# A fixed order for TensorE in an attention stage: one place a unit, transposes between projection steps

## The chip, the cores and the metric

The kernel runs on one core of a Trainium2 chip. The metric is the device time of one execution in microseconds (us); the figure of a kernel is the median of several executions. A profile is of one further execution, with its own time; its span runs from the first to the last instruction.

## The reference, cut to what matters

A trunk of two layers over 512 tokens of 1024 channels: a Mamba-2 mixer with a gated feed-forward, then differential attention with the same kind of feed-forward. The change lies in the attention alone:

```python
kv = rms_norm(x, kv_ln_g) @ kv_w                      # keys: 8 heads x 2 maps x 64; values: 8 x 128
k  = rms_norm(k, k_norm_g)
q  = rms_norm((rms_norm(x, ln_g) @ q_w).reshape(b, s, 8, 2, 64), q_norm_g)
for each block i of 128 queries, causal:
    logits = einsum('bqhcd,bkhd..', q, k) * scale + rel_bias[bucket(distance)]
    p = softmax(logits)
    attn = p[:, :, 0] - lam * p[:, :, 1]
    o = attn @ v
o = rms_norm(o, subln_g) * (1 - lam_init)
x = x + o @ attn_out_w
```

## The kernel before

The activations lie channel by token in `xgh[k]` and `xgl[k]` (k = 0 to 7, 128 channels each): every large product is made of three matmuls, high part by high, high by low and low by high, of 128 x 128 weights with 512 columns. Six projections, `k0 q0 v0 k1 q1 v1`, make the keys, queries and values of heads 0 to 3 (`0`) and 4 to 7 (`1`), and two output projections, `attn_out(0)` and `attn_out(1)`, bring the heads back into the stream. `proj` (L937) makes one projection for four blocks of 128 tokens, in four accumulators (the tag `mm` in PSUM, four banks), over four chunks of weights of two k each: 24 matmuls a chunk, 96 in all. `chunk` has the weights loaded (SyncE's queue) and split into high and low part (ScalarE and VectorE) two chunks ahead. For keys and queries, `qk` (L962) evacuates the blocks on ScalarE, squares and sums them, takes `rsqrt_act` (VectorE, ScalarE, VectorE), multiplies (L977, VectorE), and transposes the product on TensorE (`turned`, L980: 16 transposes, four a block), from which ScalarE writes `kT` or `qT` (L985).

The attention itself goes by units: a head has three, the query blocks 0 and 1 together, block 2, block 3. A unit has four steps. `logits` (L1009): matmuls of 64 rows for both maps into two banks, VectorE adds the bias and takes the maximum (L1034), ScalarE the exponential (L1042). `weigh` (L1045): VectorE makes the difference of the two maps. `turn` (L1058): TensorE transposes it into one bank, ScalarE copies it (`at`, L1064). `values` (L1066): TensorE multiplies with `vt` into one bank (`po`), ScalarE scales it into `ot` (L1077). Behind a head's last unit come `normed_out` (L1080: square, sum, `rsqrt_act`, product, L1087) and `turned_out` (L1089: four transposes into one bank `oT`, from which ScalarE makes `oh` and VectorE `ol`, L1097, the operands of the output projection). The small outputs share the tag `aux`, four banks.

What sets the order: the program is a tape. A planner orders each engine's instructions by when it holds them to be ready, with the program's order as preference, and hands out the banks of a tag as they come free. `heads` (L1101) is a generator that puts unit t's logits, unit t-2's transposes and unit t-3's values in one round, with a `yield` after each; `weave` runs projection or output steps (a step is 12 matmuls of a projection, or 12 of an output projection) at these yields. There are two runs of `heads`, over heads 0 to 3 and 4 to 7; the first runs empty before the second starts. Transposes of keys, queries and heads' outputs are put off into a list `pend` and issued by `pended`, behind the last matmul traced (`tc.issue_after`): for keys and queries inside the next projection, at its second chunk after two blocks, that is behind 36 matmuls. The bias table (`rb`, `oh`, `ps_rb`, L920 to L931) is traced ahead of all this; its buffers are those of the feed-forward before.

Of the kernel before, what the change touches and what calls it, by code (L numbers as in the profile page):

```python
# [39 lines left out]
def trunk_kernel(ctx: ExitStack, tc, x, ssm_ln_g, ssm_in_w, ssm_conv_w, ssm_conv_b, ssm_dt_bias,  # L40
# [16 lines left out]
    def mm_bank(name):  # L57
        return pp.tile([P, T], F32, tag="mm", name=name)
# [128 lines left out]
    def chunk(key):  # L187
        while state["next"] <= state["use"] + AHEAD and state["next"] < len(plan):
            emit_chunk()
        state["use"] += 1  # L190
        k, h, l = ready.pop(0)
        assert k == key, (k, key)
        return h, l

    def mm3(ps, wh, wl, xh, xl, start, stop):
        pe.matmul(ps, wh, xh, start=start, stop=False)  # L196
        pe.matmul(ps, wh, xl, start=False, stop=False)  # L197
        return pe.matmul(ps, wl, xh, start=False, stop=stop).ins  # L198
# [260 lines left out]
    def run(gen):  # L459
        for _ in gen:  # L460
            pass
# [438 lines left out]
    norm1 = Norm(bp, "f1")  # L900
    with tc.tile_pool(name="att_o", bufs=1) as op_, tc.tile_pool(name="att", bufs=1) as ap:
        rts = []
        pend = []

        def pended(age=0):

            with tc.issue_after(state["last"]):
                for p in list(pend):
                    if p[0] >= age:
                        pend.remove(p)  # L910
                        p[1]()
                    p[0] += 1

        def put_off(f):
            pend.append([0, f])


        rb = ap.tile([32, AH], F32, name="rb")
# [18 lines left out]
        def proj(key, evac):  # L937
            pss = [mm_bank("ps_%s_%d" % (key, b)) for b in range(NT)]
            for k0 in range(0, KB, 2):
                wh, wl = chunk("%s_%d" % (key, k0))  # L940
                for b in range(NT):
                    ts = slice(b * P, (b + 1) * P)
                    for k in range(k0, k0 + 2):
                        st, sp_ = k == 0, k == KB - 1
                        pe.matmul(pss[b], xgh[k][:, ts], wh[:, k - k0, :], start=st, stop=False)
                        pe.matmul(pss[b], xgh[k][:, ts], wl[:, k - k0, :], start=False, stop=False)
                        state["last"] = pe.matmul(pss[b], xgl[k][:, ts], wh[:, k - k0, :],
                                                  start=False, stop=sp_).ins
                    if b == 1:
                        if k0 == 2:  # L950
                            pended()
                        yield
                if k0 + 2 < KB:
                    yield
                if not rts:
                    tc.keep_in_program_order(act.preload_act_table_set("natural_log_exp_and_others"))
                    rts.append(norm_kv.col())
            for b in range(NT):
                evac(b, pss[b], rts[0])
            yield  # L960

        def qk(key, dst, gcol):  # L962
            kn, ss = [], ap.tile([P, NT, 8], F32, tag="qss", name="ss" + key, bufs=2)

            def evac(b, ps, rt):
                t = ap.tile([P, T], F32, tag="kn", name="kn%s_%d" % (key, b), bufs=4)
                s = ap.tile([P, T], F32, tag="ksq", name="ksq%s_%d" % (key, b), bufs=1)
                act.activation(t, ps, AF.Copy, scale=rt[:, b:b + 1])
                act.activation(s, t, AF.Square)
                dve.reduce_sum(ss[:, b, :], s.rearrange("p (a q) -> p a q", a=8), axis=AX.X)  # L970
                kn.append(t)

            yield from proj(key, evac)
            rsqrt_act(ss, ap, key, [P, NT, 8], 64)
            for b in range(NT):
                v = kn[b].rearrange("p (a q) -> p a q", a=8)
                dve.tensor_tensor(out=v, in0=v, in1=ss[:, b, :].unsqueeze(2).to_broadcast([P, 8, 64]),  # L977
                                  op=ALU.mult)

            def turned():  # L980
                for b in range(NT):
                    ps = aux_bank("kt%s_%d" % (key, b))
                    for h in range(4):
                        pe.transpose(ps[:, h * P:(h + 1) * P], kn[b][:, h * P:(h + 1) * P], ident)
                    act.activation(dst[:, :, b * P:(b + 1) * P], ps.rearrange("p (h t) -> p h t", h=4),  # L985
                                   AF.Copy, scale=c2[:, gcol:gcol + 1])

            put_off(turned)
            yield

        def vproj(key, i):
            def evac(b, ps, rt):
# [87 lines left out]
        def normed_out(h, st):  # L1080
            ot = st["ot"]
            sq = ap.tile([P, T], F32, tag="ksq", name="osq%d" % h, bufs=1)
            so = ap.tile([P, NT], F32, tag="so", name="so%d" % h, bufs=2)
            act.activation(sq, fl(ot), AF.Square)
            dve.reduce_sum(so, sq.rearrange("p (a q) -> p a q", a=NT), axis=AX.X)
            rsqrt_act(so, ap, "o%d" % h, [P, NT], P)
            dve.tensor_tensor(out=ot, in0=ot, in1=so.unsqueeze(2).to_broadcast([P, NT, P]), op=ALU.mult)  # L1087

        def turned_out(h, st):  # L1089
            ot = st["ot"]  # L1090
            ps = aux_bank("oT%d" % h)
            for i in range(NT):
                pe.transpose(ps[:, i * P:(i + 1) * P], ot[:, i, :], ident)
            oh_ = op_.tile([P, T], F32R, tag="oh", name="oh%d" % h, bufs=6)
            ol_ = op_.tile([P, T], F32R, tag="ol", name="ol%d" % h, bufs=6)
            act.activation(oh_, ps, AF.Copy, scale=c2[:, 50:51])
            dve.scalar_tensor_tensor(out=ol_, in0=ps, scalar=c2[:, 50:51], in1=oh_.bitcast(F32),  # L1097
                                     op0=ALU.mult, op1=ALU.subtract)
            return oh_, ol_

        def heads(hs, os):  # L1101

            us = []
            for h in hs:
                st = {}
                us += [Unit(h, part, st) for part in range(len(PARTS))]
            n = len(us)
            for t in range(n + 4):
                pended(1)
                if t < n:  # L1110
                    us[t].logits()
                    yield
                if 0 <= t - 1 < n:
                    us[t - 1].weigh()
                if 0 <= t - 2 < n:
                    us[t - 2].turn()
                    yield
                if 0 <= t - 3 < n:
                    us[t - 3].values()
                    yield  # L1120
                if 0 <= t - 4 < n and us[t - 4].part == len(PARTS) - 1:
                    normed_out(us[t - 4].h, us[t - 4].st)
                    put_off(lambda u=us[t - 4]: os.append(turned_out(u.h, u.st)))
                    yield

        def attn_out(i, os, norm):
            held = []
            for c in range(4):
                wh, wl = chunk("ao%d_%d" % (i, c))
                late = (2, 0, 0, 0)[c] if i else 0  # L1130
                pss = [mm_bank("ps_ao%d_%d" % (i, 2 * c + j)) for j in range(2)]

                def part(j, ks, c=c, wh=wh, wl=wl, pss=pss):
                    for k in ks:
                        state["last"] = mm3(pss[j], wh[:, k, j * P:(j + 1) * P], wl[:, k, j * P:(j + 1) * P],
                                            os[k][0], os[k][1], k == 0, k == 3)
                    if 3 in ks:
                        add_to_stream(2 * c + j, pss[j], 24, norm)
                        yield


                for j in range(late):
                    run(part(j, range(3)))
                    held.append(part(j, (3,)))
                if late:
                    pended()
                    yield from chain(*held)
                for j in range(late, 2):
                    yield from part(j, range(4))

        run(qk("k0", kT[0], 48))
        run(qk("q0", qT[0], 49))
        os0, os1 = [], []
        vp0, vp1 = vproj("v0", 0), vproj("v1", 1)
        for _ in range(3):
            next(vp0)
        lead_in(hs := heads(range(0, 4), os0), vp0, 2)
        weave(hs, chain(qk("k1", kT[1], 48), qk("q1", qT[1], 49)), 1, 2)
        for _ in range(3):
            next(vp1)  # L1160
        lead_in(hs := heads(range(4, 8), os1), vp1, 2)
        weave(hs, attn_out(0, os0, None), 1, 4)
        run(attn_out(1, os1, norm1))

    ffn(1, norm1, bp, None, None)

# [35 lines left out]
```

## Time and profile before

| | |
|---|---|
| time, median of 3 | 1359.11 us (1358.94 to 1359.96) |
| the profiled execution | 1358.49 us, of it span 1356.3 us |
| TensorE matmul, busy of the span | 1347.7 us (99%), 6421 instructions |
| TensorE weight load | 1096.4 us (81%) |
| VectorE | 913.0 us (67%) |
| ScalarE | 653.7 us (48%) |
| GpSimd | 91.2 us (7%) |
| attention stage | 743.2 to 988.2 us of the span |

The times are of one core, so its span is the kernel's. The shares are means over stages with different limits. Matmuls of a busy TensorE overlap: one of 512 columns is recorded as 0.39 us long, and the next starts before its end.

### The profile page before, as it was taken

Reading aid. Unit: us, or ns where it says so; the run is one execution under the profiler, and the core shown is the slowest. Engines: PE = TensorE matmul, PEld = TensorE weight load, DVE = VectorE, ACT = ScalarE, POOL = GpSimd, SP = SyncE. Lnnn points to the kernel's source line nnn. Section 1 sums busy time; section 2 is a strip of 40 time slices with the busy share of each in tenths; the row PEclk is TensorE's granted clock in tenths of the full one; section 3 lists DMA queues with packets and bytes.
Section 4 is the critical chain, followed back from the end, with each engine's and each line's share of the span. In section 5 each row is a group of like instructions: output and inputs, shape, how many; then the busy total and the mean of one; then the engine's idle time right before and its main releaser. Section 6 shows DMA issues by size and latency. Waiting matters only on the chain.

```text
span 1356.3 us, 16866 instructions
## 1 busy us (share of the span) xinstructions
PE 1347.7 (99%) x6421; PEld 1096.4 (81%) x6421; DVE 913.0 (67%) x1527; ACT 653.7 (48%) x1066; POOL 91.2 (7%) x118
## 2 busy tenths in 40 slices
PE   9999999999999999999999999999999999999998
PEld 7877887887888888888888877777788888888887
DVE  5989788688877774367755556767777773367742
ACT  5696744652444442234434556767664442134420
POOL 4230301100010000000002000000110000000000
PEclk9999999999999999999999999999999999999999
DMA  7452433532333333333323322221223333333322
GB/s 203 141 167 78 148 109 94 147 94 71 94 93 94 94 105 97 93 94 99 96 84 112 118 79 82 74 78 55 63 81 91 103 99 94 93 100 102 94 93 78
DMA packets 179904, 135.06 MB, mean 100 GB/s; under 512 B 6508, under 2 KB 163632, under 8 KB 179824
## 3 DMA queue, kind: packets, MB, share of 16 engines
q1 hardware_dynamic: 174048, 120.84, 30.1%
q0 software_dynamic: 4496, 12.05, 3.0%
q8 instruction: 50, 0.82, 0.3%
q10 hardware_dynamic: 1280, 1.10, 0.2%
q14 instruction: 30, 0.25, 0.1%
HBM read 131.72 MB, written 2.25 MB: 99 GB/s over the span
## 4 chain that ended last, share of the span: by engine, by line
PE 93%; DVE 3%; ACT 2%; issue 1%; DMA 0%; SPq 0%; DVEq 0%; ACTq 0%
PE ps_g L197 6%; PE ps_g L196 6%; PE ps_g L198 6%; PE ps_u L198 6%; PE ps_u L196 6%; PE ps_u L197 6%; PE ps_in L197 5%; PE ps_in L198 5%; PE ps_in L196 5%; PE ps_d L854 3%; PE ps_d L196 3%; PE ps_d L198 3%; PE ps_d L853 3%; PE ps_d L852 3%; PE ps_d L197 3%; PE ps_o L197 2%
## 5 line engine op out<-in xcount | busy, mean ns | idle before, releaser
L196 PE MATMUL ps_u<-xgh,wh_u 128*128 128x512 f32 x352 | 137.4, 390 | 0.0
L197 PE MATMUL ps_g<-xgl,wh_g 128*128 128x512 f32 x352 | 137.1, 389 | 0.0
L196 PE MATMUL ps_g<-xgh,wh_g 128*128 128x512 f32 x352 | 137.0, 389 | 0.0
L198 PE MATMUL ps_u<-xgh,wl_u 128*128 128x512 f32 x352 | 137.0, 389 | 0.0
L198 PE MATMUL ps_g<-xgh,wl_g 128*128 128x512 f32 x352 | 137.0, 389 | 0.0
L197 PE MATMUL ps_u<-xgl,wh_u 128*128 128x512 f32 x352 | 136.9, 389 | 0.0
L197 PE MATMUL ps_in<-xgl,wh_in 128*128 128x512 f32 x304 | 120.9, 398 | 0.0
L196 PE MATMUL ps_in<-xgh,wh_in 128*128 128x512 f32 x304 | 120.8, 397 | 0.0
L198 PE MATMUL ps_in<-xgh,wl_in 128*128 128x512 f32 x304 | 119.5, 393 | 0.0
L151 DVE TENSOR_TENSOR wl_d<-wr_d,wh_d 128x1024 fp32r<-128x1024 f32 (+1 forms) x46 | 54.2, 1178 | 96.9 <-ACT wh_d L147 96.7
L147 ACT ACTIVATE wh_d<-wr_d 128x1024 fp32r<-128x1024 f32 (+1 forms) x46 | 47.1, 1024 | 130.6 <-PE ps_d L854 62.4
L876 ACT ACTIVATE hh<-vg 128x512 fp32r<-128x512 f32 x44 | 27.8, 632 | 114.9 <-DVE vg L875 114.9
L824 DVE TENSOR_TENSOR uu<-ps_u,nr_f 128x512 f32<-128x512 f32 x44 | 30.4, 691 | 78.0 <-PE ps_u L198 77.9
L197 PEld LDWEIGHTS ps_g<-xgl,wh_g 128*128 128x128 f32 x352 | 66.2, 188 | 14.1 <-DVE xgl L414 0.3
L198 PEld LDWEIGHTS ps_u<-xgh,wl_u 128*128 128x128 f32 x352 | 66.0, 188 | 13.9
L198 PEld LDWEIGHTS ps_g<-xgh,wl_g 128*128 128x128 f32 x352 | 66.1, 188 | 13.7
L196 PEld LDWEIGHTS ps_u<-xgh,wh_u 128*128 128x128 f32 x352 | 66.2, 188 | 13.5
L196 PEld LDWEIGHTS ps_g<-xgh,wh_g 128*128 128x128 f32 x352 | 66.0, 187 | 13.6
L197 PEld LDWEIGHTS ps_u<-xgl,wh_u 128*128 128x128 f32 x352 | 66.0, 188 | 13.5
L147 ACT ACTIVATE wh_g<-wr_g 128x1024 fp32r<-128x1024 f32 x44 | 46.7, 1062 | 51.6 <-PE ps_u L197 32.3
L198 PE MATMUL ps_d<-hh,wl_d 128*128 128x512 f32 x176 | 68.5, 389 | 0.0
L196 PE MATMUL ps_d<-hh,wh_d 128*128 128x512 f32 x176 | 68.5, 389 | 0.0
(347 smaller groups left out, 3169.6 us busy)
## 6 DMA issues: line engine op xcount, KB each, us to landing
wr_g<-in_ffn_up_w_dram SPq DMA_DIRECT2D x44, 512.0 KB, 3.9
wr_u<-in_ffn_up_w_dram SPq DMA_DIRECT2D x44, 512.0 KB, 3.9
wr_d<-in_ffn_down_w_dram SPq DMA_DIRECT2D x42, 512.0 KB, 3.6
wr_in<-in_ssm_in_w_dram SPq DMA_DIRECT2D x40, 512.0 KB, 3.9
m<-cumd POOLq DMA_DIRECT2D x16, 512.0 KB, 4.6
wr_out<-in_ssm_out_w_dram SPq DMA_DIRECT2D x16, 512.0 KB, 3.5
wr_k<-in_kv_w_dram SPq DMA_DIRECT2D x8, 512.0 KB, 4.1
wr_q<-in_q_w_dram SPq DMA_DIRECT2D x8, 512.0 KB, 3.9
```

The costliest lines, as they stand in the source:

```text
L147: return act.activation(self.wh[:, :self.n], self.raw[:, :self.n], AF.Copy)
L151: return dve.tensor_tensor(out=self.wl[:, :self.n], in0=self.raw[:, :self.n], in1=self.wh[:, :self.n].bitcast(F32), op=ALU.subtract)
L196: pe.matmul(ps, wh, xh, start=start, stop=False)
L197: pe.matmul(ps, wh, xl, start=False, stop=False)
L198: return pe.matmul(ps, wl, xh, start=False, stop=stop).ins
L824: dve.tensor_tensor(out=u, in0=ps, in1=r, op=ALU.mult)
L852: pe.matmul(pss[b], hh[k][:, ts], wh[:, k - k0, :], start=k == 0, stop=False)
L853: pe.matmul(pss[b], hh[k][:, ts], wl[:, k - k0, :], start=False, stop=False)
L854: pe.matmul(pss[b], hl[k][:, ts], wh[:, k - k0, :], start=False, stop=k == n - 1)
L876: act.activation(h, ga, AF.Copy)
```

## The change

TensorE's instructions of the attention are traced inside `tc.manual_schedule(engines={PE})`: they are issued in the order in which the program has them. The other engines are still ordered by the planner. That order is written out:

- One run over all 24 units instead of two over 12. In round t, unit t-2's transposes, unit t's logits and unit t-3's values stand together, one place, with 1 + 2 + 1 banks; then follow `steps[t]` steps of the filling work, the chain `v0, k1, q1, v1, attn_out(0)`.
- A step of a projection is two blocks of one chunk, 12 matmuls. A step of `attn_out(0)` is two parts of three matmuls, 6 matmuls; the first two accumulators wait with their last part (the head 3 one).
- `normed_out` of a head is traced directly behind its last values; `turned_out` stands after the first step of a later round.
- Keys' and queries' transposes go in pairs of blocks, the first pair behind 24 matmuls of the next projection, the second behind 36. The evacuation is traced by pairs too, behind the last step of the two blocks.
- `last_out`: three of four parts of two accumulators (18 matmuls), the last head's transposes, two parts (6 matmuls) of the third accumulator, and then the rest.

`Unit.logits`, `weigh`, `turn`, `values`, `normed_out` and `turned_out` stay as they are. The diff, without the lines that it takes away of `pended`, `heads` and the former `attn_out`, which are printed above:

```diff
--- before.py
+++ after.py
@@ -900,19 +900,7 @@
     norm1 = Norm(bp, "f1")
     with tc.tile_pool(name="att_o", bufs=1) as op_, tc.tile_pool(name="att", bufs=1) as ap:
         rts = []
...
+        late = []
 
 
         rb = ap.tile([32, AH], F32, name="rb")
@@ -944,20 +932,19 @@
                         st, sp_ = k == 0, k == KB - 1
                         pe.matmul(pss[b], xgh[k][:, ts], wh[:, k - k0, :], start=st, stop=False)
                         pe.matmul(pss[b], xgh[k][:, ts], wl[:, k - k0, :], start=False, stop=False)
-                        state["last"] = pe.matmul(pss[b], xgl[k][:, ts], wh[:, k - k0, :],
-                                                  start=False, stop=sp_).ins
-                    if b == 1:
-                        if k0 == 2:
-                            pended()
+                        pe.matmul(pss[b], xgl[k][:, ts], wh[:, k - k0, :], start=False, stop=sp_)
+                    if b % 2:
+                        if (k0, b) in ((0, 3), (2, 1)) and late:
+                            late.pop(0)()
+                        if k0 == 0 and b == 3:
+                            if not rts:
+                                tc.keep_in_program_order(
+                                    act.preload_act_table_set("natural_log_exp_and_others"))
+                                rts.append(norm_kv.col())
+                        if k0 + 2 == KB:
+                            for i in (b - 1, b):
+                                evac(i, pss[i], rts[0])
                         yield
-                if k0 + 2 < KB:
-                    yield
-                if not rts:
-                    tc.keep_in_program_order(act.preload_act_table_set("natural_log_exp_and_others"))
-                    rts.append(norm_kv.col())
-            for b in range(NT):
-                evac(b, pss[b], rts[0])
-            yield
 
         def qk(key, dst, gcol):
             kn, ss = [], ap.tile([P, NT, 8], F32, tag="qss", name="ss" + key, bufs=2)
@@ -977,16 +964,16 @@
                 dve.tensor_tensor(out=v, in0=v, in1=ss[:, b, :].unsqueeze(2).to_broadcast([P, 8, 64]),
                                   op=ALU.mult)
 
-            def turned():
-                for b in range(NT):
+            def turned(bs):
+                for b in bs:
                     ps = aux_bank("kt%s_%d" % (key, b))
                     for h in range(4):
                         pe.transpose(ps[:, h * P:(h + 1) * P], kn[b][:, h * P:(h + 1) * P], ident)
                     act.activation(dst[:, :, b * P:(b + 1) * P], ps.rearrange("p (h t) -> p h t", h=4),
                                    AF.Copy, scale=c2[:, gcol:gcol + 1])
 
-            put_off(turned)
-            yield
+            late.append(lambda: turned((0, 1)))
+            late.append(lambda: turned((2, 3)))
 
         def vproj(key, i):
             def evac(b, ps, rt):
@@ -1098,69 +1085,91 @@
                                      op0=ALU.mult, op1=ALU.subtract)
             return oh_, ol_
 
...
+        os = []
+
+        def attn_out(i, norm, ms):
+
+            pss, ws = {}, {}
+
+            def part(m, k):
+                if m not in pss:
+                    if m % 2 == 0:
+                        ws[m // 2] = chunk("ao%d_%d" % (i, m // 2))
+                    pss[m] = mm_bank("ps_ao%d_%d" % (i, m))
+                w = ws[m // 2]
+                cols = slice(m % 2 * P, (m % 2 + 1) * P)
+                mm3(pss[m], w[0][:, k, cols], w[1][:, k, cols], *os[4 * i + k], k == 0, k == 3)
+                if k == 3:
+                    add_to_stream(m, pss[m], 24, norm)
+
+            todo = [(m, k) for m in ms for k in range(4)]
+            if ms[0] == 0:
+
+                todo[:8] = [(m, k) for ks in (range(3), (3,)) for m in range(2) for k in ks]
+            for n, mk in enumerate(todo):
+                part(*mk)
+                if n % 2:
+                    yield
+
+        def last_out(norm):
+
+            w = chunk("ao1_0")
+            pss = [mm_bank("ps_ao1_%d" % m) for m in range(2)]
+
+            def part(m, ks):
+                for k in ks:
+                    cols = slice(m * P, (m + 1) * P)
+                    mm3(pss[m], w[0][:, k, cols], w[1][:, k, cols], *os[4 + k], k == 0, k == 3)
+
+            part(0, range(3))
+            part(1, range(3))
+            while late:
+                late.pop(0)()
+            rest = attn_out(1, norm, range(2, KB))
+            next(rest)
+            for m in range(2):
+                part(m, (3,))
+                add_to_stream(m, pss[m], 24, norm)
+            run(rest)
+
+        with tc.manual_schedule(engines={mybir.EngineType.PE}):
+            run(qk("k0", kT[0], 48))
+            run(qk("q0", qT[0], 49))
+            fill = chain(vproj("v0", 0), qk("k1", kT[1], 48), qk("q1", qT[1], 49), vproj("v1", 1),
+                         attn_out(0, None, range(KB)))
             us = []
-            for h in hs:
+            for h in range(AH):
                 st = {}
                 us += [Unit(h, part, st) for part in range(len(PARTS))]
             n = len(us)
...
+
+            steps = [2] * 13 + [1, 1, 1] + [2, 1, 2, 1, 2, 1, 2] + [2, 1, 1, 1]
+            ots = []
+            for _ in range(3):
+                next(fill)
+            for t in range(n + 3):
+                if 0 <= t - 2 < n:
+                    us[t - 2].turn()
                 if t < n:
                     us[t].logits()
-                    yield
-                if 0 <= t - 1 < n:
+                    if t:
+                        us[t - 1].weigh()
+                elif t == n:
                     us[t - 1].weigh()
-                if 0 <= t - 2 < n:
-                    us[t - 2].turn()
-                    yield
                 if 0 <= t - 3 < n:
...
+                    u = us[t - 3]
+                    u.values()
+                    if u.part == len(PARTS) - 1:
+                        normed_out(u.h, u.st)
+                        ots.append([t + 1, u])
+                for i in range(steps[t]):
+                    next(fill)
+                    if i == 0 and ots and ots[0][0] <= t and (steps[t] > 1 or t > n):
+                        u = ots.pop(0)[1]
+                        os.append(turned_out(u.h, u.st))
+            assert next(fill, None) is None
+            late.append(lambda: os.append(turned_out(AH - 1, us[-1].st)))
+            last_out(norm1)
 
     ffn(1, norm1, bp, None, None)
```

## Rows read from the trace of the kernel before

**Rows 1.** The page, part 4, the chain that ended last by engine.

```profile
PE 93%; DVE 3%; ACT 2%; issue 1%; DMA 0%; SPq 0%; DVEq 0%; ACTq 0%
```

**Rows 2.** Windows: attention stage, its last part (us, busy us by engine, clock, DMA).

```profile
743.20:988.20 245.00, 242.93 (x1241) 189.95 (x1240) 164.96 (x438) 155.66 (x353) 8.93 (x6) 1.00 0.26 79
919.50:966.00 46.50, 45.32 (x259) 34.13 (x259) 36.91 (x116) 31.99 (x91) 0.00 (x0) 1.00 0.15 46
```

**Rows 3.** Timeline of TensorE: projections and transposes (start us, us, instruction).

```profile
766.99 0.39 PE L945 MATMUL ps_q<-wh_q,xgh 128*128 128x512 f32 x1
...
775.16 1.91 PE L984 MATMUL ktk<-ident,knk 128*128 128x128 f32 x16
776.82 0.48 PE L945 MATMUL ps_q<-wh_q,xgh 128*128 128x512 f32 x1
...
790.53 0.39 PE L945 MATMUL ps_v<-wh_v,xgh 128*128 128x512 f32 x1
```

**Rows 4.** Timeline of TensorE: logits and values.

```profile
801.50 0.50 PE L945 MATMUL ps_v<-wh_v,xgh 128*128 128x512 f32 x1
...
807.20 0.92 PE L1028 MATMUL lg<-kT,qT 64*128 64x384 f32 x4
808.05 0.50 PE L945 MATMUL ps_v<-wh_v,xgh 128*128 128x512 f32 x1
...
813.73 1.13 PE L1028 MATMUL lg<-kT,qT 64*128 64x512 f32 x4
814.79 0.50 PE L945 MATMUL ps_v<-wh_v,xgh 128*128 128x512 f32 x1
...
838.48 0.93 PE L1028 MATMUL lg<-kT,qT 64*128 64x128 f32 x8
839.34 0.55 PE L1063 MATMUL at<-ident,lg 128*128 128x128 f32 x3
...
876.58 1.06 PE L1074 MATMUL po<-vt,at 128*128 128x128 f32 x8
877.39 0.48 PE L945 MATMUL ps_q<-wh_q,xgh 128*128 128x512 f32 x1
```

**Rows 5.** Groups by line and shape, TensorE, attention stage (count, busy, mean ns).

```profile
L1074 PE MATMUL po<-vt,at 128*128 128x128 f32 x160 | 22.3, 278 | 1.7 <-DVE ol L1097 1.5
```

**Rows 6.** List of waits of TensorE; timeline of TensorE behind an output transpose.

```profile
PE po L1074 <- DVE ol L1097: 1.5, 2, 0.8
...
852.35 0.55 PE L1063 MATMUL at<-ident,lg 128*128 128x128 f32 x3
853.66 1.16 PE L1074 MATMUL po<-vt,at 128*128 128x128 f32 x8 [0.77 <-DVE ol L1097]
```

**Rows 7.** Timeline: products for the key transposes, VectorE; end of k1, TensorE.

```profile
771.91 2.50 DVE L977 TENSOR_TENSOR knk<-knk,ssk 128x512 f32<-128x512 f32 x4
...
850.09 0.83 PE L1074 MATMUL po<-vt,at 128*128 128x128 f32 x6
...
858.18 2.49 DVE L977 TENSOR_TENSOR knk<-knk,ssk 128x512 f32<-128x512 f32 x4
```

**Rows 8.** Timeline: last values of heads 4 and 7, and their normed ot.

```profile
928.77 1.06 PE L1074 MATMUL po<-vt,at 128*128 128x128 f32 x8
...
937.81 0.68 DVE L1087 TENSOR_TENSOR ot<-ot,so 128x512 f32<-128x512 f32 x1
...
965.74 0.47 PE L196 MATMUL ps_ao<-oh,wh_ao 128*128 128x512 f32 x1
...
969.08 0.69 DVE L1087 TENSOR_TENSOR ot<-ot,so 128x512 f32<-128x512 f32 x1
```

**Rows 9.** Timeline: table of the bias requested, SyncE, and used, TensorE.

```profile
743.86 0.87 SPq L925 DMA_DIRECT2D oh<-onehot_dram  x2
...
747.08 1.23 PE L927 MATMUL ps_rb<-oh,rb 32*8 32x320 f32 x4
```

More of the change, by code (lines that the diff above doesn't have):

```diff
@@ L902, in trunk_kernel @@
         rts = []
[L903 to L915, printed above, removed]
+        late = []
         rb = ap.tile([32, AH], F32, name="rb")
@@ L1099, in turned_out @@
             return oh_, ol_
-        def heads(hs, os):
+        os = []
[40 more added lines that the diff above has]
+                         attn_out(0, None, range(KB)))
             us = []
-            for h in hs:
+            for h in range(AH):
                 st = {}
@@ L1107, in heads @@
             n = len(us)
-            for t in range(n + 4):
-                pended(1)
+            steps = [2] * 13 + [1, 1, 1] + [2, 1, 2, 1, 2, 1, 2] + [2, 1, 1, 1]
[5 more added lines that the diff above has]
+                    us[t - 2].turn()
                 if t < n:
                     us[t].logits()
-                    yield
-                if 0 <= t - 1 < n:
+                    if t:
+                        us[t - 1].weigh()
+                elif t == n:
@@ L1114, in heads @@
                     us[t - 1].weigh()
-                if 0 <= t - 2 < n:
-                    us[t - 2].turn()
-                    yield
                 if 0 <= t - 3 < n:
[L1119 to L1163, printed above, removed]
+                    u = us[t - 3]
```

## The prediction

> **What bounds the kernel now.** I read the page first, from the top: the chain of work that ended last is TensorE's for 93% of the span [rows 1], so a microsecond taken from TensorE's own sequence is a microsecond of the time. Then I cut out the attention stage with the view by windows, from the first `ps_k` matmul to the last `ps_ao` one: 245.0 us, TensorE busy in 242.9 of them at a granted clock of 1.00, VectorE in 165.0 and ScalarE in 155.7 [rows 2]. A busy TensorE is not one at its peak, because its matmuls overlap; what a matmul costs is the distance from its start to the next start. So I read the timeline of TensorE and priced by distances.
>
> A projection or output matmul (128x512): 36 of them from 766.99 to 775.16 are 8.17 us, 0.227 each. Sixteen transposes take 1.66 us, 0.104 each. The run of 60 projection matmuls after them takes 13.71 us where 60 x 0.227 is 13.62: coming back from small matmuls costs about 0.10 [rows 3]. Logits of one unit take 0.86 (blocks 0 and 1), 0.85 (block 2) and 1.06 (block 3); the 24 projection matmuls between two logits take 5.70, 0.25 more than 24 x 0.227; 0.10 of this is the way back, so logits add 0.15, of which I put 0.10 on going into them and 0.05 on going from them straight to a projection. Eight `po` matmuls ahead of a projection take 0.81, as much each as the transposes [rows 4].
>
> With these prices the stage's work is: 768 large matmuls (six projections of 96, two outputs of 96) x 0.227 = 174.3; logits 8 heads x (0.86 + 0.85 + 1.06) = 22.2; small ones 80 `at` + 160 `po` [rows 5] + 64 key and query transposes + 32 output transposes = 336 x 0.104 = 34.9; the bias table 1.2 and the norm's four transposes 0.4. Sum 233.0. The stage takes 245.0, so 12.0 us are switches and waits. This is all that an order of TensorE can win.
>
> The waits that a row names are two of the same make: transposes of a unit take 1.31 us to the next start where three should take 0.33, and the `po` behind them waits for `ol` (1.5 us in the list of waits, twice 0.98 by the distances): an output transpose was put directly ahead of a unit, took one of the four aux banks, and the bank came back only when VectorE had read it [rows 6].
>
> The Trainium skill, page "Perfetto Trace Analysis", section "Identifying the Most-Contended Engine", holds that matmul busy time says little of the distance to the roofline and that the busy share of weight loads does. By that rule the stage has 245.0 - 190.0 = 55 us of room, and a new order could win several times what I count; the distances here give 12.0, and the trace does not bear the 55 out, since large matmuls start every 0.227 us with nothing between them.
>
> **The change, part by part.** No arithmetic is added or removed; matmuls, evacuations and loads are the same in number. Only places in a queue move.
>
> (1) *One place a unit.* Turn, logits and values of three units stand together, 27 places. Ways back to a large matmul: 27 places + 8 key/query pairs + 8 output transposes + bias table + norm, less the two pairs that lie directly ahead of a place (the second of `q0` and the second of `q1`) = 43, x 0.10 = 4.3. Logits are entered 24 times, x 0.10 = 2.4. No row shows logits followed by `po`; followed by `at` they take their 0.86, so I take nothing (bounds: 0 to 0.05 x 24 = 1.2). Together 6.7 us of switches, against 12.0 us of switches and waits: 5.3 us less, if nothing waits. The waits of [rows 6] go because the output transpose now has at least six output matmuls (1.4 us) behind it before the next place, and 1.2 us more of that place pass before its fourth bank is wanted.
>
> (2) *Key and query transposes earlier.* The first pair stands after 24 matmuls of the next projection, where it stood after 36. `k0` ends at 766.99, so the pair would start at 766.99 + 5.45 = 772.44. The products it reads come from VectorE, four in 2.50 us from 771.91, the first done at about 772.6, the second at 773.2, with 0.44 us of transposes between [rows 7]. Wait: about 0.4 for `k0` and as much for `q0`, which has no unit between either. Bounds 0 (if ScalarE's and VectorE's queues put the pieces of weights that now lie in this chain behind it) and 1.3 each. I take 0.8 together. For `k1` and `q1` one unit's place lies between: 2.8 + 2.1 + 2.8 = 7.7 us after the projection's end. Now the first product of `k1` is done some 8.7 us after it (850.09 to 858.8), amid unit work [rows 7]. Bounds 0 and 1.3 each; I take 0.4 each, since the row lies near the upper part and the evacuation of the first two banks now starts half a step sooner: 0.8.
>
> (3) *Output transposes between steps.* The chain from the last `po` of a head to the normed `ot` takes 4.0 us when nothing is in the way (965.74 to 969.77) and 8.7 us at worst (about 929.8 to 938.5) [rows 8]. Head 0 to 3 get 10 us or more; head 5 about 9.6, head 6 about 7.6, head 7 about 5.4. Head 4 gets least: one step of 1.4, a place of 2.1, one step of 1.4 = 4.9. Bounds 0 and 3.8; VectorE is less crowded at that point than at the worst, so I take 0.4.
>
> (4) *Evacuations of a projection by pairs, heads 3 to 4 without a drain, weights' order.* TensorE had large matmuls under all of these before and has now; they cost nothing as long as the four mm banks are free, and each bank's reader (0.69 us) has three other blocks' 4 us of matmuls over it.
>
> Sum: -5.3 + 0.8 + 0.8 + 0.4 = -3.3 us. The profiled execution took 1358.49 (span 1356.3 and 2.2 around it), so 1355.2 on that run's scale; the median of the runs shown is 0.6 higher, so I say 1355.8, 0.24% less than 1359.11. A measurement of this kernel can tell about 0.2%, 2.7 us, from no change.
>
> **Rivals.** *Forecast:* faster, 1352.5 to 1356.4 (from no new wait at all, 1359.1 - 5.3 = 1353.8, less 1.3 if the 43 ways back cost 0.03 less than read, to the point where 2.7 us are still gained). Chance 0.52.
>
> *The last part is paced by VectorE and ScalarE.* From 919.5 to 966.0 VectorE is busy 36.9 of 46.5 us and ScalarE 32.0 [rows 2], and they wait for each other in turn (logits' maximum, exponentials, weighing). That part is 2.5 us shorter in my sum. With TensorE's order fixed it cannot pass by a late unit. If the ping-pong keeps its 46.5, and the waits of (2) and (3) come, 2.5 of the 3.3 us are lost: about 1358.3, no change. For it: 79% busy there already. Against it: every unit has two full places between logits and turn, as now. Chance 0.20.
>
> *The bias table is held in front.* Its matmuls stand ahead of the block whose order is fixed. Now the planner puts them at 747.08, 16 matmuls into `k0`, because their table is requested only at 743.86, when the feed-forward's buffers are free [rows 9]. If the fixed order also puts them ahead of the block's first matmul, TensorE stands from 743.2 to about 746.9: +3.7, about 1359.5, no change. Chance 0.10.
>
> *Slower: each late unit stops TensorE.* Until now the planner could put the next projection step where a unit's transposes would have waited. If the four banks or the weighing come late by 0.4 us at each of the 24 units (VectorE waits about that for the exponentials of each unit), 9.6 us are added to my sum: about 1365. It decides from 0.25 us a unit, where the 3.3 us are gone and 2.7 more. For it: banks are exactly four a place; against it: the only named waits now come from a fifth bank. Chance 0.18.
>
> Faster 0.52, same 0.30, slower 0.18. With the tenth of the fast side below 1352.5 and the far slow cases left out, the range is 1352.0 to 1361.5; for the likeliest case alone 1352.5 to 1356.4.
>
> **What would show it.** Right: the stage near 241.7 us, no `po` waiting for `ol`, 43 runs of large matmuls, small waits of `ktk`/`ktq` for VectorE's product. Wrong: `lg`, `at` or `po` waiting for VectorE or ScalarE at many places between 919 and 966 (the slow rival), `ps_rb` ahead of the first `ps_k` with idle time before it, or an `oT` of head 4 that holds TensorE for 2 us or more. I would be wrong upward if no chain were late at all.

## The result, and the profile after

The changed kernel takes 1361.80 us (median of 14 executions, 1360.41 to 1363.61) against 1358.99 us before (14, 1358.27 to 1359.96): ratio 1.0022, with a 95% interval of [1.0013, 1.0030] (later ratios are to the kernel before in the same way). It is slower by 2.8 us, where 3.3 us less were forecast, and lies 0.3 us above the range.

The profiled execution took 1362.95 us, 4.5 more than that of before. The windows say where: up to the first `ps_k` 744.6 us (before 743.2), the attention stage 248.05 (245.00 in [rows 2]), the rest 368.15 (368.10). The 1.4 us ahead of the stage are none of the change: the code there is the same, and in this one execution TensorE waited 1.7 us for the first loads of `x` (0.6 before) and 0.5 for `gacc` (no such wait before). In the ten other profiles of this case the first `ps_k` starts between 742.81 and 743.84. The stage's 3.05 us agree with the medians.

The list of TensorE's waits, whose two rows of the attention are (total us, times, longest):

```profile
PE oT L1080 <- DVE rc L1036: 3.6, 1, 3.6
...
PE ktq L971 <- DVE knq L964: 0.2, 1, 0.2
```

The `po` wait of [rows 6] is gone. In its place a single output transpose waits 3.6 us. (The list names `rc`, the instruction behind the product on VectorE; what the transpose reads is the product `ot`, done at 936.17.) TensorE's timeline there (start, us, instruction, idle time before it):

```profile
931.09 0.48 PE L196 MATMUL ps_ao<-oh,wh_ao 128*128 128x512 f32 x1
...
932.33 0.40 PE L198 MATMUL ps_ao<-oh,wl_ao 128*128 128x512 f32 x1
936.31 0.69 PE L1080 MATMUL oT<-ident,ot 128*128 128x128 f32 x4 [3.58 <-DVE rc L1036]
936.69 0.74 PE L196 MATMUL ps_ao<-oh,wh_ao 128*128 128x512 f32 x1
937.23 0.63 PE L197 MATMUL ps_ao<-ol,wh_ao 128*128 128x512 f32 x1
...
938.93 0.63 PE L198 MATMUL ps_ao<-oh,wl_ao 128*128 128x512 f32 x1
939.36 0.99 PE L1050 MATMUL at<-ident,lg 128*128 128x128 f32 x4
940.28 0.92 PE L1015 MATMUL lg<-kT,qT 64*128 64x384 f32 x4
```

This is head 4. Six output matmuls, from 931.09, have 5.22 us to the next start where the same six take 1.48 elsewhere: 3.74 us of waiting. Then a second cost. The six from 936.69 take 2.67 us, 0.43 from start to start instead of 0.23, and four `at` take 0.92 instead of 0.53. Together 1.6 us. The windows of the same stretch have the cause in the column behind POOL's, the granted clock:

```profile
744.60:992.65 248.05, 244.16 (x1242) 190.65 (x1241) 165.06 (x438) 156.27 (x353) 8.95 (x6) 0.99 0.26 78
931.09:932.60 1.51, 1.51 (x9) 1.03 (x7) 1.51 (x10) 0.88 (x5) 0.00 (x0) 1.00 0.00 0
932.60:936.30 3.70, 0.13 (x1) 0.02 (x1) 3.67 (x12) 2.85 (x10) 0.00 (x0) 1.00 0.02 4
936.30:939.40 3.10, 3.09 (x11) 2.44 (x12) 1.70 (x4) 0.69 (x1) 0.00 (x0) 0.57 0.54 174
939.40:945.00 5.60, 5.60 (x30) 3.56 (x29) 2.65 (x9) 2.76 (x7) 0.00 (x0) 0.93 0.00 0
```

Ahead of the stop the clock is 1.00 (2.4 GHz), behind it 0.57 over 3.1 us, which is nearly all at the lower level of 1.2 GHz. One place costs 3.7 + 1.6 = 5.3 us. The list of waits shows two thirds of that.

Why the `ot` was late: in the window of the wait VectorE is busy 3.67 of 3.70 us. Its timeline, and ScalarE's, for head 4's chain:

```profile
927.95 0.37 ACT L1064 ACTIVATE ot<-po,rc 128x128 f32<-128x128 f32 x1 [1.60 <-PE po L1061]
...
929.83 0.61 ACT L1071 ACTIVATE osq<-ot 128x512 f32<-128x512 f32 x1
```

```profile
931.08 0.68 DVE L1072 TENSOR_REDUCE so<-osq 128x4 f32<-128x512 f32 x1
...
932.86 0.16 DVE L438 TENSOR_TENSOR rst_o<-so 128x4 f32<-128x4 f32 x1
932.93 0.69 DVE L511 TENSOR_TENSOR xT<-ps_ao,xT 128x512 f32<-128x512 f32 x1
933.53 0.15 DVE L439 SCALAR_TENSOR_TENSOR rst_o<-rst_o,rsm_o 128x4 f32<-128x4 f32 x1
...
933.67 0.69 DVE L511 TENSOR_TENSOR xT<-ps_ao,xT 128x512 f32<-128x512 f32 x1
934.27 0.15 DVE L440 SCALAR_TENSOR_TENSOR so<-rst_o,so 128x4 f32<-128x4 f32 x1
934.34 1.22 DVE L151 TENSOR_TENSOR wl_ao<-wr_ao,wh_ao 128x1024 fp32r<-128x1024 f32 x1
935.48 0.69 DVE L1074 TENSOR_TENSOR ot<-ot,so 128x512 f32<-128x512 f32 x1
```

From the last scaled `ot` (927.95) to the normed one (936.17) are 8.2 us. About 4.4 of them are other work let in between the chain's own small instructions: ScalarE's exponentials ahead of the square (1.5), a weighing ahead of the sum (0.6), two additions to the stream `xT` (0.6 each), and the split of a weight chunk, `wl_ao`, ahead of the last product (1.1).

### The profile page after: what moved, and what is told of

Its sections match the earlier page's. It is cut to its first block, busy times and chain, and to the rows that moved or that the text cites. A ratio compares the mean times of both kernels' runs of the same rounds, so it can differ in the third digit from the quotient of the medians.

```text
span 1360.8 us, 16862 instructions
## 1 busy us (share of the span) xinstructions
PE 1348.9 (99%) x6421; PEld 1097.0 (81%) x6421; DVE 914.7 (67%) x1527; ACT 654.7 (48%) x1066; POOL 91.8 (7%) x118
## 4 chain that ended last, share of the span: by engine, by line
PE 94%; DVE 2%; ACT 2%; issue 1%; DMA 1%; POOL 0%; SPq 0%; DVEq 0%; ACTq 0%
PE ps_g L197 6%; PE ps_g L198 6%; PE ps_g L196 6%; PE ps_u L198 6%; PE ps_u L196 6%; PE ps_u L197 6%; PE ps_in L197 5%; PE ps_in L198 5%; PE ps_in L196 5%; PE ps_d L852 3%; PE ps_d L197 3%; PE ps_d L198 3%; PE ps_d L854 3%; PE ps_d L853 3%; PE ps_d L196 3%; PE ps_o L196 2%
## 5 line engine op out<-in xcount | busy, mean ns | idle before, releaser
L197 PE MATMUL ps_d<-hl,wh_d 128*128 128x512 f32 x176 | 68.5, 389 | 0.0
```

## The experiments

**Head 4's output transposes later, and nothing else.**

```diff
-                        ots.append([t + 1, u])
+                        ots.append([t + (3 if u.h == 4 else 1), u])
```

> The changed kernel with one edit: head 4's output transposes stand one two-step round later (round 20 instead of 18). Theory A (one late chain: TensorE stood 3.6 us for head 4's normed output, and ran 8 matmuls at the low clock behind it): the wait goes, granted clock 1.00 throughout, 5.5 us less than the changed kernel, about 1356.3 (before 1359.0). Rival B (with TensorE's order fixed, the last part is paced by VectorE and ScalarE, so a removed wait comes back at the next places): at least half of the 5.5 us comes back as waits of lg, at or po, about 1359 to 1361.

Measured: 1357.42 us (1356.83 to 1358.17), ratio 0.9990 [0.9982, 0.9999]: 4.4 us less than the changed kernel. Its windows, the stage and its part from the first output matmul on, and TensorE's timeline:

```profile
743.10:986.60 243.50, 242.79 (x1241) 189.53 (x1241) 164.69 (x438) 155.94 (x353) 8.90 (x6) 1.00 0.26 79
...
920.30:986.60 66.30, 65.80 (x349) 51.19 (x348) 53.65 (x134) 43.09 (x102) 7.48 (x5) 1.00 0.19 58
```

```profile
935.57 0.40 PE L198 MATMUL ps_ao<-oh,wl_ao 128*128 128x512 f32 x1
936.33 0.74 PE L1050 MATMUL at<-ident,lg 128*128 128x128 f32 x3 [0.35 <-DVE lg L1042]
...
938.06 1.16 PE L1061 MATMUL po<-vt,at 128*128 128x128 f32 x8
938.97 0.48 PE L196 MATMUL ps_ao<-oh,wh_ao 128*128 128x512 f32 x1
...
961.86 1.06 PE L1061 MATMUL po<-vt,at 128*128 128x128 f32 x8
962.67 0.48 PE L196 MATMUL ps_ao<-oh,wh_ao 128*128 128x512 f32 x1
```

The stop and the low clock are gone, and the stage is 1.5 us shorter than before the change. So one of the eight places of output transposes made the loss. VectorE is still full when the last units come: the next unit's transposes start 0.5 us late (936.33) and run apart, 0.67 us where three take 0.42, and the logits at 942.71 take 1.07 instead of 0.86, 1.0 us in all. The two `po` rows show a term that the prediction put at nothing: eight `po` behind logits take 0.91 us to the next start, behind transposes 0.81; likewise six take 0.69 and 0.59.

**The norm's chain ahead on VectorE and ScalarE, place unchanged.**

```diff
-                        normed_out(u.h, u.st)
+                        with tc.high_priority():
+                            normed_out(u.h, u.st)
```

> The changed kernel with TensorE's order untouched; only the planner is told to prefer the instructions of normed_out (square, sum, root, product) to others that are ready. Theory A1 (the 8.2 us of head 4's chain are queueing: 4.2 us of its 8.2 were other instructions on VectorE and ScalarE ahead of its own): oT of head 4 waits under 1 us, no low clock, 1356.5 to 1357.5. Rival A2 (the chain itself is too long for the 4.9 us, whatever the order): oT still waits 2 us or more, 1360 to 1362.

Measured: 1358.18 us (1357.74 to 1359.72), ratio 0.9998 [0.9989, 1.0007].

```profile
932.63 0.63 PE L1080 MATMUL oT<-ident,ot 128*128 128x128 f32 x4 [0.99 <-DVE mx L1024]
933.01 0.48 PE L196 MATMUL ps_ao<-oh,wh_ao 128*128 128x512 f32 x1
```

```profile
932.60:936.00 3.40, 3.37 (x19) 2.38 (x20) 3.29 (x7) 3.03 (x10) 0.00 (x0) 1.00 0.04 11
```

The transposes stand in the same place, and their wait falls from 3.6 to 1.0 us because the chain is shorter: from the last scaled `ot` to the normed one it takes 5.6 us (926.86 to 932.49) instead of 8.2. So 2.6 us of the wait came from other work let in on VectorE and ScalarE; the last 1.0 stays even with the chain ahead, since the place itself is early. Behind a stop of 1.0 us the window from 932.6 to 936.0 has a granted clock of 1.00. The time is 3.6 us less than the changed kernel's: 2.6 of waiting and the clock's 1.6, less some small new waits (a `po` waits 0.2 for `ol` here); by the profiles the stage is 3.8 shorter.

**Head 4's output transposes one step later (six matmuls).**

```diff
-                    if i == 0 and ots and ots[0][0] <= t and (steps[t] > 1 or t > n):
+                    if i == (1 if t == 18 else 0) and ots and ots[0][0] <= t and (steps[t] > 1 or t > n):
```

> The changed kernel, with head 4's output transposes behind the second step of round 18 instead of the first, so six output matmuls (1.4 us) later; nothing else. This parts the two halves of what the stop cost there: 3.9 us of waiting and about 1.7 us in which the granted clock was lower behind it. Theory (the place alone is too early, the chain to the normed ot does not depend on it): the wait falls by the 1.4 us, from 3.6 to 2.2. If the low clock follows the shorter wait as well, 1361.8 - 1.4 = 1360.4 us, and the transposes, logits and values behind it are seen at a clock below 1.00. If it does not, 1361.8 - 1.4 - 1.7 = 1358.7 us. Rival (the chain is itself held by work that TensorE's next place feeds, so it is later too): the wait stays near 3.6 us and the time at 1361.8 us.

Measured: 1359.01 us (1358.62 to 1361.01), ratio 1.0003 [0.9994, 1.0012]. The ten times lie in two groups, and each has one of the two expected values: six from 1358.62 to 1359.07 us, all with a mean granted clock of 1.000, and four from 1360.25 to 1361.01, with 0.998 or 0.999. Between the middles of the groups are 1.6 us (1358.84 and 1360.43). The profiled execution is of the second group:

```profile
933.16 0.39 PE L198 MATMUL ps_ao<-oh,wl_ao 128*128 128x512 f32 x1
935.77 1.09 PE L1080 MATMUL oT<-ident,ot 128*128 128x128 f32 x4 [2.21 <-DVE rc L1036]
936.65 1.06 PE L1050 MATMUL at<-ident,lg 128*128 128x128 f32 x4
937.64 1.65 PE L1015 MATMUL lg<-kT,qT 64*128 64x384 f32 x4
939.22 0.94 PE L1061 MATMUL po<-vt,at 128*128 128x128 f32 x6
```

```profile
935.70:939.22 3.52, 3.45 (x13) 2.08 (x13) 1.73 (x5) 1.28 (x2) 0.00 (x0) 0.52 0.45 154
939.22:945.00 5.78, 5.78 (x34) 4.35 (x33) 4.21 (x14) 2.82 (x8) 0.00 (x0) 1.00 0.00 0
```

The wait falls by 1.4 us to 2.2, as the theory has it; the rival (a chain that moves with TensorE) falls. The low clock met other instructions and cost the same: four `oT` 0.88 instead of 0.35, four `at` 0.99 instead of 0.53, logits 1.58 instead of 0.85, together 1.7 us. Of the changed kernel's 14 executions eight have a mean clock of 0.998 or less, which no recorded execution of the kernel before has; five more have 0.999, which tells nothing by itself, as some executions of the kernel before have it too.

**Keys' and queries' transposes in one place**, on top of the first experiment.

```diff
-                        if (k0, b) in ((0, 3), (2, 1)) and late:
+                        if (k0, b) == (2, 1) and late:
...
-            late.append(lambda: turned((0, 1)))
-            late.append(lambda: turned((2, 3)))
+            late.append(lambda: turned(range(NT)))
```

> As the run before, and all four blocks' key and query transposes stand together behind 36 matmuls of the next projection, as in the kernel before. Theory A: the waits for VectorE's products in k0 and q0 (about 0.4 and 0.5 us in the profile of the changed kernel) go, k1 and q1 had none, four returns to large matmuls less at 0.04: 0.9 to 1.1 us less than e1, about 1355.3. Rival B (the pairs relieve the aux banks and ScalarE later on): as e1 or up to 1 us slower.

Measured: 1356.97 us (1356.43 to 1358.65), ratio 0.9988 [0.9979, 0.9997]; 0.45 less than without the edit, half of what the theory said, with overlapping ranges. The changed kernel's timeline has these waits at the first pair of `k0`:

```profile
773.61 0.39 PE L935 MATMUL ps_q<-wh_q,xgl 128*128 128x512 f32 x1
774.07 1.26 PE L971 MATMUL ktk<-ident,knk 128*128 128x128 f32 x8
775.09 0.48 PE L933 MATMUL ps_q<-wh_q,xgh 128*128 128x512 f32 x1
```

The pair starts 0.46 us after the matmul ahead of it, where 0.23 is usual, and takes 1.02 where the second takes 0.79: 0.46 us late in all. `q0` gives 0.5 in the same way. At `k1` and `q1` no pair is late. Without the pairs these waits are gone, and the first logits of the stage start 0.8 us earlier than in the first experiment. But most of that is lost again where a place stands directly behind sixteen transposes:

```profile
862.06 1.49 PE L1014 MATMUL lg<-kT,qT 64*128 64x512 f32 x4
863.48 1.16 PE L1060 MATMUL po<-vt,at 128*128 128x128 f32 x8
```

These logits take 1.42 us to the next start, and 1.14 behind a pair in the first experiment; at `q1` it is 1.21 instead of 0.93. By the profiles the stage is 0.2 us shorter. So the theory has the waits right, and the rival (the pairs relieve what comes later) tells why so little of them is won.

**TensorE ordered by the planner, with the text of the change.**

```diff
-        with tc.manual_schedule(engines={mybir.EngineType.PE}):
+        if True:
```

> The changed kernel without the fixed order: the planner orders TensorE too, from the same program text. Theory A: the planner moves ready matmuls ahead of head 4's transposes where it holds them late, 1356.5 to 1359. Rival C (the text's places are what costs, not that they are fixed): the wait of oT stays at 3 us or more, 1361 to 1363.

Measured: 1356.36 us (1355.95 to 1357.27), ratio 0.9981 [0.9972, 0.9990], the best of all runs. Around head 4 its timeline has

```profile
933.91 0.39 PE L198 MATMUL ps_ao<-oh,wl_ao 128*128 128x512 f32 x1
934.47 0.63 PE L1080 MATMUL oT<-ident,ot 128*128 128x128 f32 x4 [0.18 <-DVE rc L1036]
934.94 0.60 PE L1050 MATMUL at<-ident,lg 128*128 128x128 f32 x4
...
937.14 0.49 PE L1050 MATMUL at<-ident,lg 128*128 128x128 f32 x3
...
939.58 0.47 PE L196 MATMUL ps_ao<-oh,wh_ao 128*128 128x512 f32 x1
```

The planner set 15 more output matmuls ahead of the late transposes (21 from 929.26 on) and two places with none between them behind. In the planner's hands the text of the change wins 2.4 us against the kernel before; fixed as written it loses 2.8, and 4.4 of the 5.4 us between the two are head 4's place, by the first experiment.

**The planner's order with one place for keys' and queries' transposes** (both edits above).

> The text of the changed kernel with TensorE ordered by the planner (no fixed order), and the four blocks' transposes of keys and queries in one place, behind 36 matmuls, as in the kernel before. Theory (pairs cost a wait of some 0.4 us at k0 and at q0 and one more way back to large matmuls each, in whichever order): 0.4 to 0.8 us less than the 1356.4 us of the planner's order with pairs, so 1355.6 to 1356.0 us. Rival (the planner already puts the first pair later where it would wait, so nothing is left): 1356.4 us.

Measured: 1356.38 us (1356.12 to 1357.14), ratio 0.9981 [0.9972, 0.9990]: the same as with pairs. The profiled stage is shorter (242.3 against 242.8 us), but the times don't bear a gain out: the time is the rival's. Its reason is not: with one place the first logits start 1.2 us earlier here too, and half of it is lost behind the sixteen transposes of `k1` and `q1`.

**Fixed order with all three edits** (head 4 later, one place, chain first).

> The changed kernel, TensorE's order fixed, with the three single edits together: head 4's output transposes two rounds later, keys' and queries' transposes in one place, and a head's norm ahead of the units' work on VectorE and ScalarE. Theory (the stop at head 4 is gone with the later place, and the chain's rank then matters no more): as with the first two alone, 1357.0 us within 0.4. Rival 1 (the norm's rank takes away what is left of the waits of transposes and logits, about 0.9 us): 1356.1 us. Rival 2 (ranked first, the norm holds up the weighing of a unit, and a unit's transposes wait for it): 1358 us or more, with waits of at for lg in the list of waits.

Measured: 1357.19 us (1356.42 to 1358.03), ratio 0.9987 [0.9978, 0.9996]. As the theory has it: with the place late enough the chain's rank adds nothing to be measured.

**Logits last in each place**, on top of the first experiment.

```diff
+                if 0 <= t - 3 < n:
+                    us[t - 3].values()
                 if t < n:
                     us[t].logits()
...
                     u = us[t - 3]
-                    u.values()
```

> The changed kernel with head 4's output transposes two rounds later (as in the run of that alone, 1357.42 us) and in each place the order transposes, values, logits instead of transposes, logits, values; TensorE's order is fixed. It tests the term that the prediction put at nothing: logits followed by values. By the distances of that run, eight values behind logits take 0.91 us and behind transposes 0.81, six take 0.69 and 0.59: 0.10 at each of 21 places, 2.1 us. Theory (the price lies in leaving logits for small matmuls, and going from logits to a large one costs 0.02 to 0.03 more than from values): a place costs 0.09 us less, so the stage is 1.9 us shorter and the time 1355.5 us; values take 0.59 and 0.81 where transposes stand ahead. Rival 1 (the price is only moved, from logits-to-values to values-to-logits and logits-to-large): within 0.4 of 1357.4 us. Rival 2 (logits 0.6 us later in each place make the maximum, the exponentials and the weighing later, and transposes wait for them): over 1357.4 us, with waits of at for lg.

Measured: 1362.22 us (1361.58 to 1363.27), ratio 1.0024 [1.0014, 1.0034]. The theory falls: rival 1 has the price, rival 2 the time. A clean place, and three of the waits:

```profile
871.04 0.49 PE L1050 MATMUL at<-ident,lg 128*128 128x128 f32 x3
871.37 0.83 PE L1061 MATMUL po<-vt,at 128*128 128x128 f32 x6
872.13 0.93 PE L1015 MATMUL lg<-kT,qT 64*128 64x128 f32 x8
872.99 0.50 PE L933 MATMUL ps_q<-wh_q,xgh 128*128 128x512 f32 x1
```

```profile
PE po L1061 <- ACT vt L980: 1.2, 1, 1.2
...
PE lg L1015 <- DVE ol L1084: 0.9, 1, 0.9
PE at L1050 <- DVE lg L1042: 0.8, 1, 0.8
```

Transposes 0.33, values 0.76, logits 0.86: 1.95 us, where the other order takes 0.42 + 0.86 + 0.69 = 1.97. Going into logits from values costs 0.17, and the other order paid 0.09 to enter them from transposes and 0.10 to leave them for values: the price is only moved. And values that stand earlier wait for `vt` of the projection before, logits that stand later wait for a bank and make their unit late. With the pairs of `k1` and `q1`, which are late here too, the late places add up to 5.8 us by distances, where the first experiment has 1.0: the 4.8 us by which this run is slower than that one. No stop here is over 1.2 us, and the profile's granted clock is 1.000.

**The same in the planner's order.**

> The planner's order with keys' and queries' transposes in one place (1356.38 us in its own run), and in the program's order values ahead of logits in each place. Theory (the price of going from logits to values goes, as with the fixed order): 1356.4 - 1.9 = 1354.5 us, the fastest so far. Rival (the planner orders the place by its own due times and puts values behind logits again, or logits later make other work late): 1356.4 us or more.

Measured: 1358.21 us (1357.59 to 1359.06), ratio 0.9996 [0.9987, 1.0005], 1.8 us more than with logits ahead of values; `oT` waits 0.9 us and `po` for `vt` 0.4.

## Why the prediction was wrong

*The step that failed is (3), the output transposes of head 4.* It took 0.4 us of the bounds 0 and 3.8, because "VectorE is less crowded at that point than at the worst". The worst row, 8.7 us in [rows 8], was head 4's own, with the same output projection and a weight split beside it; the changed kernel's chain took 8.2. That row is the upper bound, 3.8, and the wait measured 3.7; nothing in the trace spoke for a tenth of it. Of the signs that the prediction named, "an `oT` of head 4 that holds TensorE for 2 us or more" is the one that came.

*A cost that no term held.* The 1.6 us at the lower clock are behind that wait and beyond the bound of 3.8; with them the place costs 5.3 us, more than the 3.3 us to be won. The Trainium skill, page "TensorE: Matmul & The Clock Gate", section "HAM oscillation — how this bites in real kernels", has TensorE go on at the lower rate behind a wait (there for a DMA, here for VectorE). The trace agrees for the stop of 3.6 us, with 1.6 us lost; behind the stop of 2.2 us it came in four executions of ten, with 1.7 us lost in the profiled one.

*Step (1) was right in what it removed and short in one price.* The named waits of [rows 6] went, ways back to large matmuls are 41 in the trace (43 said), most of them at 0.10 to 0.14 (0.10 said), and going into logits costs 0.09 (0.10 said). Going from logits to `po` was put at nothing, bounds 0 and 1.2; it costs 0.10 at each of 21 places, 2.1 us.

*Step (2) was right for `k0` and `q0`* (0.46 and 0.5 for 0.4 each) and too high for `k1` and `q1` (no wait for 0.4 each). The first product of `k1` is done 7.8 us after the projection's end (850.91 to 858.66), not 8.7 as in [rows 7], and the pair stands 8.1 us behind it, not 7.7, since output transposes (0.35) went in between.

With these the forecast for the stage, 241.7 us, becomes 241.7 - 0.4 + 5.3 + 2.1 + 0.2 - 0.8 = 248.1; the profile has 248.05. That it comes so close is partly luck: 41 ways back at about 0.12 are 4.9 us where 4.3 were reckoned, and values behind transposes (0.59 and 0.81) take 0.7 us less in all than at the 0.104 a matmul of the sum.

*Step (4)* holds: no large matmul waits in the stage for an evacuation or a weight.

*The rivals.* The last part as a whole is not paced by VectorE and ScalarE: with head 4's place moved, TensorE's late places there come to 1.0 us in all. What their crowding did cost came at one place, as head 4's late chain. (The length of the part says less: from the first output matmul to the stage's end it is 68.8 us before and 66.3 in the first experiment, but one unit's logits, transposes and values have moved ahead of it and head 3's output transposes into it, which is some 1.5 us of the difference.) The bias table was not held in front: `ps_rb` stands 16 matmuls into `k0` again. "Each late unit stops TensorE" had the right side by the wrong mechanism: the 24 units are not late by 0.4 each, one transpose is late by 3.7. The gain itself was there, though smaller: with that one place moved the same order wins 1.4 us by the medians taken together (1357.42 against 1358.79), and 2.4 with the planner's order.

What stays open: why the low clock follows a stop of 2.2 us in four executions of ten and not in the others, and how far the 1.0 us of waits left in the first experiment could be taken out by a third place for head 4.

## What to carry to other kernels

A hand-written order for one engine is safe only where each operand's chain is priced with what shares its engines, so take the longest chain that the profile shows for that very operand, or leave the engine's planner the freedom to pass over a late instruction. One place that is too early can cost more than a whole regrouping wins, so look for the single longest wait before judging an order. And price a change of order by every neighbouring pair that it makes new, since 0.1 us at 21 places was 2.1 of the 5.3 us that the regrouping was to win.

## What the runs showed of the hardware that was not expected

- Behind a stop of TensorE of 3.6 us, with 1.00 granted until then, the granted clock was 0.57 over the next 3.1 us and the kernel lost 1.6 us more; behind one of 2.2 us four of ten executions lost as much by their times, and the one of them that was profiled had 0.52 over 3.5 us; behind stops of 1.0 us (chain first) and 1.2 us (logits last) the clock of the profile stayed at 1.00.
- Logits (64 rows) among transposes and values (128 rows) cost 0.17 to 0.19 us for going in and out, in either order, while values directly behind transposes cost nothing more: 0.59 us for six, 0.81 for eight, 0.10 each.
